# The recurrence's values by Strassen's scheme in a hybrid layer

## The chip, the core and the metric

One core of a Trainium2 chip runs the whole layer in one launch. It has a matrix engine (PE, with its weight loads shown as PEld), a vector engine (DVE), an activation engine (ACT), GpSimd (POOL), a queue engine that issues DMAs (SP), and 16 DMA engines. The metric is device microseconds from start to end, the median of several runs.

## The reference

The layer takes x of 512 tokens by 1024 channels, in float32. What matters here:

```python
h = rms_norm(x, norm_g); P = h @ W_in     # q | f | i | z_a | c_q | c_kv | k_rope | z_b | gates
f = lb + (1 - lb) * sigmoid(hf);  k = 1 - f;  v = hi            # hi = h @ W_I, 1024 columns
S_t = diag(f_t) S_{t-1} + k_t v_t^T;  o_t = S_t^T silu(q_t)     # 8 heads of 128, chunks of 32
y_a = rms_norm(o) * silu(z_a)
y_b = causal attention from the low-rank c_q, c_kv, k_rope, times silu(z_b)
m = sigmoid(g_a) * (y_a @ W_pa) + sigmoid(g_b) * (y_b @ W_pb)
out = rms_norm(x + m @ W_out)
```

The change concerns v = h @ W_I, a product of 512x1024 by 1024x1024.

## The kernel before

**Products.** Every operand of PE is split into a high and a low half (float32r), and a product is three matmuls into one bank of PSUM: hi by hi, hi by lo, lo by hi (`mm3`, L102 to L104). PE's left-hand data are h transposed, kept as two tiles `hT`. Weights come through `load_w` (L110 to L131): a DMA on SP's queue into one of three raw buffers, a cast to the high half on ACT (L129), a subtraction for the low half on DVE (L130); the high and low halves have four buffers each. PSUM's eight banks of 128x512 are two pools: three `mm` banks for projections and five `ax` banks for the rest.

**Stages.** RMS norm and transposes of x; the low-rank projections c, 256 columns during the norm and 448 after it (to 45 us); then four pairs of heads of the recurrence; then attention over eight heads; then the merge gates, the two projections and the output, which already use Strassen's scheme on 2x2 blocks (L898, L1096). For these, sums of weight blocks are made by DMA: `BlockSums` copies blocks in DRAM (`queued`, one copy behind each weight load) and adds others to them by accumulating DMAs on POOL (L800), one pair of them at each `step()`. Sums of token blocks of h are made by `early_sums` on DVE in pair 0 and saved to DRAM.

**A pair** (`hg_pair`) projects f for two heads (24 matmuls of 512 a head), and for each head runs `hg_forget`: tanh `tf` on ACT (L463), `f` on DVE (L464), `fr` and `k` on POOL (L465, L466), a scan (L468) and a reciprocal (L469) on DVE. The reciprocal takes the only buffer of `tf`, so the next head's `tf` must wait until `ki` (L486) has read it. `ko` (L487), `k64` on POOL (L488) and `k128` (L489) follow; `k128` is transposed on PE (L512) and used with the values for the states (L521, L522, L525). Then q's projection, scores (L535 to L546, masked on DVE at L550), outputs (L559, L561), the head's norm (L565 to L567) and the gate z_a. A pair with an even number first projects the values of four heads, 512 columns, by `proj_tok`: 4 token tiles of 8 x 3 matmuls, each tile copied by ACT (L603). So the values of all heads take 2 x 96 matmuls, in pair 0 and in pair 2.

**Order.** A scheduler in the framework orders each engine's instructions; each engine then runs its own list strictly in order. `tc.issue_after` holds an instruction behind another one. The low-rank tiles `c_sb` are transposed on PE (L425, 20 transposes into five ax banks), scaled by ACT (L426) and split by DVE (L427), within pair 0's forget projection.

## Time and profile before

| | us |
|---|---|
| median of 3 runs | 609.78 (609.2 to 610.34) |
| the profiled execution | 609.93 |
| its span | 607.7 |
| PE busy | 598.3 (98%) |
| DVE busy | 436.6 (72%) |
| ACT busy | 286.2 (47%) |
| POOL busy | 146.4 (24%) |

The difference between the profiled execution and its span, 2.2 us, lies outside the profiled instructions. Busy shares are means over stages. A row of the groups reads: line, engine, operation, out<-in with shapes, count, then busy time in us and the mean of one in ns, then the engine's idle time ahead of them and what ended it.

### The profile page before, as it was taken

What the parts mean: (1) busy time and instruction counts of PE and PEld (TensorE: products, weight loads), DVE (VectorE), ACT (ScalarE), POOL (GpSimd) and SP (SyncE); (2) the same over time, 40 slices, a digit from 0 to 9 for tenths busy, and PEclk for the clock granted to TensorE, in tenths of its full rate; (3) what the DMA queues carried; (4) which work ended last, traced back from release to release, by engine and by line L of the source; (5) the groups of instructions that cost most, each with busy time, mean ns of one, the idle gap of its engine ahead of it and who ended that gap; (6) DMA issues with size and microseconds to landing.
All of it is one profiled execution on the core that took longest, in us unless ns stands there. A gap on an engine that the chain in (4) does not pass through costs nothing.

```text
span 607.7 us, 9766 instructions
## 1 busy us (share of the span) xinstructions
PE 598.3 (98%) x3670; PEld 524.8 (86%) x3670; DVE 436.6 (72%) x684; ACT 286.2 (47%) x533; POOL 146.4 (24%) x253
## 2 busy tenths in 40 slices
PE   8999999999999999999999999999999999999995
PEld 5998888888888888888888888899999999888884
DVE  7717989599764548959767776747757678567886
ACT  6555245333313342435646555438757854424452
POOL 3106322254350137414254530400000000000012
PEclk9999999999999999999999999999999999999998
DMA  7549479987969967573369575866665564695113
GB/s 257 177 138 345 154 218 369 320 220 171 237 151 275 220 185 147 125 172 90 57 163 169 148 152 126 237 243 198 189 184 178 195 195 160 200 347 183 61 35 139
DMA packets 74543, 114.37 MB, mean 188 GB/s; under 512 B 7512, under 2 KB 41726, under 8 KB 74496
## 3 DMA queue, kind: packets, MB, share of 16 engines
q1 hardware_dynamic: 65244, 89.95, 46.1%
q0 software_dynamic: 8336, 22.55, 19.9%
q10 hardware_dynamic: 916, 1.25, 0.6%
q8 instruction: 29, 0.48, 0.3%
q14 instruction: 18, 0.15, 0.1%
HBM read 105.34 MB, written 39.85 MB: 239 GB/s over the span
## 4 chain that ended last, share of the span: by engine, by line
PE 96%; ACT 1%; DMA 1%; DVE 0%; issue 0%; SPq 0%; POOLq 0%; POOL 0%; ACTq 0%
PE mm_ps L102 19%; PE mm_ps L104 19%; PE mm_ps L103 19%; PE ax_ps L898 16%; PE ax_ps L1096 5%; PE mm_ps L898 3%; PE mm_ps L283 2%; PE ax_ps L757 1%; PE ax_ps L731 1%; PE ax_ps L559 1%; PE mm_ps L1096 1%; PE ax_ps L561 1%; PE ax_ps L521 1%; DMA w_raw<-w_in 1%; PE ax_ps L104 1%; PE ax_ps L103 1%
## 5 line engine op out<-in xcount | busy, mean ns | idle before, releaser
L130 DVE TENSOR_TENSOR w_lo<-w_raw,w_hi 128x1024 fp32r<-128x1024 f32 (+3 forms) x116 | 138.3, 1205 | 68.3 <-ACT w_hi L129 65.4
L129 ACT CAST w_hi<-w_raw 128x1024 fp32r<-128x1024 f32 (+3 forms) x116 | 115.1, 1005 | 130.1 <-PE mm_ps L103 56.5
L102 PE MATMUL mm_ps<-hT,w_hi 128*128 128x512 f32 x320 | 125.8, 394 | 0.0
L103 PE MATMUL mm_ps<-hT,w_hi 128*128 128x512 f32 x320 | 125.3, 391 | 0.0
L104 PE MATMUL mm_ps<-hT,w_lo 128*128 128x512 f32 x320 | 125.2, 393 | 0.0
L104 PEld LDWEIGHTS mm_ps<-hT,w_lo 128*128 128x128 f32 x320 | 60.1, 188 | 12.3
L102 PEld LDWEIGHTS mm_ps<-hT,w_hi 128*128 128x128 f32 x320 | 60.2, 188 | 11.9
L103 PEld LDWEIGHTS mm_ps<-hT,w_hi 128*128 128x128 f32 x320 | 60.2, 188 | 11.9
L898 PE MATMUL ax_ps<-s,w_hi 128*128 128x256 f32 x384 | 54.2, 283 | 0.2 <-ACT w_hi L129 0.2
L898 PEld LDWEIGHTS ax_ps<-s,w_hi 128*128 128x128 f32 x384 | 49.6, 192 | 0.5 <-ACT w_hi L129 0.5
L1147 POOL TENSOR_SCALAR ssum<-ssum 128x1 f32<-128x1 f32 x3 | 0.9, 309 | 188.0 <-ACT sq L1134 188.0
L103 PE MATMUL mm_ps<-w_lo,hT 128*128 128x512 f32 (+1 forms) x96 | 36.6, 383 | 0.0
L104 PE MATMUL mm_ps<-w_hi,hT 128*128 128x512 f32 (+1 forms) x96 | 36.5, 382 | 0.0
L102 PE MATMUL mm_ps<-w_hi,hT 128*128 128x512 f32 (+1 forms) x96 | 36.2, 386 | 0.0
L739 ACT ACTIVATE p<-ax_ps,sm 128x128 f32<-128x128 f32 (+3 forms) x32 | 16.7, 525 | 35.4 <-DVE sm L738 32.8
L741 POOL TENSOR_SCALAR p<-p,sm 128x128 f32<-128x128 f32 (+3 forms) x28 | 15.6, 560 | 66.2 <-DVE sm L740 54.9
L898 PE MATMUL ax_ps<-s,w_lo 128*128 128x256 f32 x192 | 31.4, 284 | 0.0
L469 DVE RECIPROCAL tf<-pr 128x512 f32<-128x512 f32 x8 | 26.8, 3348 | 0.1
L898 PEld LDWEIGHTS ax_ps<-s,w_lo 128*128 128x128 f32 x192 | 26.6, 192 | 0.2 <-DVE w_lo L130 0.2
L102 PE MATMUL mm_ps<-cT,w_hi 128*128 128x512 f32 x52 | 20.7, 397 | 0.0
L104 PEld LDWEIGHTS mm_ps<-w_hi,hT 128*128 128x128 f32 x96 | 18.0, 188 | 3.0
L102 PEld LDWEIGHTS mm_ps<-w_hi,hT 128*128 128x128 f32 x96 | 18.0, 188 | 2.9
(308 smaller groups left out, 1204.8 us busy)
## 6 DMA issues: line engine op xcount, KB each, us to landing
w_raw<-w_in SPq DMA_DIRECT2D x54, 512.0 KB, 6.4
g_t<-w_in SPq DMA_DIRECT2D x16, 512.0 KB, 9.1
w_raw<-g_t SPq DMA_DIRECT2D x16, 512.0 KB, 4.4
g_t<-w_in POOLq DMA_DIRECT2D x8, 512.0 KB, 10.5
pa_t<-w_proj_a SPq DMA_DIRECT2D x8, 512.0 KB, 8.9
g_t<-g_t POOLq DMA_DIRECT2D x8, 512.0 KB, 9.5
out_t<-w_out SPq DMA_DIRECT2D x8, 512.0 KB, 8.0
s<-h POOLq DMA_DIRECT2D x8, 512.0 KB, 11.6
```

What stands on the lines that cost most here:

```text
L102: nc.tensor.matmul(ps, lh[lsl], rh[rsl], start=start, stop=False)
L103: nc.tensor.matmul(ps, lh[lsl], rl[rsl], start=False, stop=False)
L104: nc.tensor.matmul(ps, ll[lsl], rh[rsl], start=False, stop=stop)
L129: last_hi[0] = nc.scalar.copy(hi[:, :o], raw[:, :o])
L130: last_lo[0] = nc.vector.tensor_tensor(lo[:, :o], raw[:, :o], hi[:, :o].bitcast(F32), op=ALU.subtract)
L283: nc.tensor.matmul(ps, hT[l][:, 4 * kh + k, t * P : t * P + P], c_hl[kh][r][:, k * 256 : k * 256 + 256], start=kh == 0 and kind == 0 and k ...
L469: nc.vector.reciprocal(rp[:], pr[:])
L521: nc.tensor.matmul(sps[:, sl], kt_[:, sl], v_sb[i][:, (h % 4) * P : (h % 4) * P + P], start=True, stop=True)
L739: last_act[0] = nc.scalar.activation(p[:, :n], sps[:, :n], AF.Exp, scale=SCALE, bias=sm[:, 1:2], accum_out=sm[:, 2:3])
L741: scaled_p = (nc.vector if final else nc.gpsimd).tensor_scalar(p[:, :n], p[:, :n], sm[:, 3:4], 0.5, op0=ALU.mult, op1=ALU.mult)
L898: nc.tensor.matmul(ps[:, o], w[k // 2][i][:, k % 2, cols], ap[j][:, k], start=not banks and c == 0 and n == 0, stop=n == 11, skip_group_ch ...
L1096: nc.tensor.matmul(ps[:, o : o + n], ap[i][:, k, t * P : t * P + P], w[k // 2][j][:, k % 2, o : o + n], start=fresh and c == 0, stop=c == ...
```

## The change

The values are one Strassen product now: seven products of 256x512 by 512x512, of 24 matmuls each (two token tiles, three kinds, four k), 168 instead of 192. W_I is taken in four blocks of 512x512, h in four blocks of 512 channels by 256 tokens. In pair 0 (`values_first`) there are five: U = h11 by I11; s2 by a sum of blocks and s3 by another, both added into U's banks; h12 by I21; h22 by a third sum. In pair 2 (`values_rest`) there are two: s1 by a fourth sum, then s4 by I22 into the same banks. The partial results that pair 2 needs are kept in four tiles (`v_late`). With this:

- Sums of W_I's blocks are made in SBUF, in the tile `ya` (which also holds x at the start): loads on SP, accumulating DMAs on POOL ahead of pair 0 and, for pair 2, in `RestSum` as the second step of pair 1.
- `early_sums` makes s2 and s3 on DVE ahead of the first forget projection; s1 and s4 are made in `fetch_rest`, behind pair 0's outputs on DVE.
- The first forget projection and U stand ahead of the transposes of `c_sb`, which are held behind U's first tile. The rope key's transposes move behind pair 0's states, and pairs 1 to 3 have their gate ahead of q's projection.
- Behind a weight load go up to two queued copies in pairs 0 and 1, one later, none in the last pair after its gate and at attention's first head. The block sums of the gates are added in another order, two steps a head for h > 4.

```diff
-                if queued:
+                for _ in range(min(len(queued), behind[0])):
...
+    i_w3, i_w2 = ya[:, 0:4], ya[:, 4:8]
...
+    for q in kh:
+        nc.gpsimd.dma_start(i_w3[:, q], i_w[1, 1][:, q], accum_op=ALU.add)
...
+    with tc.issue_after(c_lo_last.ins):
+        s_kept = early_sums()
+        for q in kh:
+            nc.vector.tensor_tensor(i_w2[:, q], i_w2[:, q], i_w3[:, q], op=ALU.add)
...
+    def v_product(ap, w, done, banks=None, tile=ax_tile):
+
+        res = banks or [tile() for _ in range(2)]
+        for t, ps in enumerate(res):
+            for n, (x, k) in enumerate((x, k) for x in range(3) for k in range(4)):
+                i, j = ((0, 0), (1, 0), (0, 1))[x]
+                mm_ = nc.tensor.matmul(ps[:], ap(i, k, t), w[k // 2][j][:, k % 2], start=not banks and n == 0, stop=n == 11,
+                                       skip_group_check=banks is not None)
...
+    first_f = proj_ch(w_in, COL_F, hT)
+    first_mm = []
+    first_u = v_product(h11, i_block(0, 0), lambda t, ps: first_mm.append(last_mm[0]))
...
-            nc.tensor.transpose(ps[:, t * P : t * P + P], c_sb[:, t, j * P : j * P + P], ident[:])
+            with tc.issue_after(first_mm[0].ins):
+                nc.tensor.transpose(ps[:, t * P : t * P + P], c_sb[:, t, j * P : j * P + P], ident[:])
...
+        for t, ps in enumerate(u):
+            nc.scalar.copy(v_sb[t][:], ps[:])
+        v_product(s2, i_split(i_w2), late(2), u)
+        v_product(s3, i_split(i_w3), late(3), u)
+        w10, raws = [], []
+        for q in kh:
+            w10.append(load_w(i_w[1, 0][:, q]))
+            nc.vector.tensor_tensor(i_w2[:, q], i_w2[:, q], last_raw[0].rearrange("p (k c) -> p k c", k=2), op=ALU.add)
+        v_product(h12, w10, lambda t, ps: nc.vector.tensor_tensor(v_sb[t][:], v_sb[t][:], ps[:], op=ALU.add), tile=mm_tile)
+        v_product(h22, i_split(i_w2), lambda t, ps: nc.scalar.copy(v_sb[2 + t][:], ps[:]), u)
...
+    class RestSum:
+
+        def add(self):
+            with tc.issue_after(last_pool[0].ins):
+                for q in kh:
+                    nc.gpsimd.dma_start(i_w2[:, q], i_w[0, 1][:, q], accum_op=ALU.add)
...
+    def values_rest():
+
+        def rest(n):
+            def done(t, ps):
+                nc.vector.scalar_tensor_tensor(v_sb[2 * (n - 2) + t][:], ps[:], -1.0, v_late[n, t][:], op0=ALU.mult, op1=ALU.add)
+            return done
+
+        r = v_product(of_sum(s_late[1]), i_split(i_w2), rest(3), tile=mm_tile)
+        v_product(of_sum(s_late[4]), i_block(1, 1), rest(2), r)
...
-            proj_tok(w_in, COL_I + cc, hT, lambda t, ps: nc.scalar.copy(v_sb[t][:], ps[:]))
-        else:
+            (values_rest if pair else values_first)()
+        if pair:
             zz = gate()
...
+    adds = [(gate_w[0], 0), (RestSum(),), (gate_w[0], 1), (gate_w[0], 2), (gate_w[0], 3), (gate_w[1], 0), (gate_w[1], 1),
...
         if pair == 0:
-            early_sums(kh[1])
+            with tc.issue_after(last_on[0].ins):
+                fetch_rest()
```

How the lists stand: three places, with the row's number, line, operation, out<-in. First ACT at the start of pair 0, before the change (`cT_91` is the scaled transposed low-rank tile, `v_821` to `v_824` the values).

```order
33 L129 CAST w_hi<-w_raw 128x1024 x2
34 L463 ACTIVATE tf<-mm_ps 128x512
35 L426 ACTIVATE cT_91<-ax_ps,par 128x512 x5
36 L129 CAST w_hi<-w_raw 128x1024
37 L171 CAST kpe<-ax_ps 128x512
38 L463 ACTIVATE tf<-mm_ps 128x512
39 L603 COPY v_821<-mm_ps 128x512
```

And the same place now (`ya` holds W_I's sums, `v_841` and `v_842` the values of two token tiles):

```order
37 L131 CAST w_hi<-w_raw 128x1024
38 L173 CAST w_hi<-ya 128x1024 x4
39 L526 ACTIVATE cT_91<-ax_ps,par 128x512 x5
40 L555 ACTIVATE tf<-mm_ps 128x512
41 L691 COPY v_841<-ax_ps 128x512
42 L691 COPY v_842<-ax_ps 128x512
43 L686 ACTIVATE qr<-ax_ps 128x512
```

The first tf moved from ahead of the five cT to behind them, and the copies of U's banks stand behind both. On PE the 48 matmuls of the forget projection and U's 24 now stand ahead of the 20 transposes, and the product of s2 into U's banks right behind them. On DVE four casts' low halves and two sums on `ya` stand ahead of the cT rows.

Second, POOL in pair 1 (`k_1390` and now `k_1433` are the second head's k64, `q_1536` and `q_1583` the first head's q64). Before:

```order
73 L488 TENSOR_TENSOR k_1390<-ko,gh_639 128x256
74 L800 DMA g_t_647<-w_in 128x2x512 x2
75 L502 TENSOR_TENSOR q_1536<-qi,gh_635 128x256
76 L502 TENSOR_TENSOR q_1545<-qi,gh_639 128x256
77 L800 DMA g_t_644<-g_t_643 128x1024 x2
```

Now:

```order
72 L594 TENSOR_TENSOR q_1583<-qi,gh_759 128x256
73 L580 TENSOR_TENSOR k_1433<-ko,gh_763 128x256
74 L713 DMA ya<-w_in 128x2x512 x2
75 L594 TENSOR_TENSOR q_1592<-qi,gh_763 128x256
76 L963 DMA g_t_768<-g_t_767 128x1024 x2
```

The accumulations of `RestSum` (L713) have the place that the second addition of the gates' sums had, behind the second head's k64.

Third, DVE in pair 2, whose rows between the low half of `RestSum`'s block (row 145) and the update of the values that the s4 product waits for (L742, `v_1854`) end so (`asb` are masked scores, `st` states):

```order
162 L642 COPY_PREDICATED asb_765<-mask_le,ax_ps 64x4x64
163 L617 SCALAR_TENSOR_TENSOR st<-st,ft,ax_ps 128x128
164 L132 TENSOR_TENSOR w_lo<-w_raw,w_hi 128x1024
165 L579 TENSOR_TENSOR ko<-ki,pr 128x512
166 L556 TENSOR_SCALAR f<-tf,c_425,c_427 128x512
167 L617 SCALAR_TENSOR_TENSOR st<-st,ft,ax_ps 128x128
168 L560 SCALAR_TENSOR_TENSOR pr<-f,fr 128x512
169 L561 RECIPROCAL tf<-pr 128x512
170 L742 SCALAR_TENSOR_TENSOR v_1854<-mm_ps,qh 128x512
171 L742 SCALAR_TENSOR_TENSOR v_1855<-mm_ps,p_917 128x512
```

Before, the values of pair 2 were four copies on ACT with nothing but casts between them:

```order
80 L463 ACTIVATE tf<-mm_ps 128x512
81 L603 COPY v_1805<-mm_ps 128x512
82 L603 COPY v_1806<-mm_ps 128x512
83 L129 CAST w_hi<-w_raw 128x1024 x3
84 L603 COPY v_1807<-mm_ps 128x512
85 L603 COPY v_1808<-mm_ps 128x512
```

The update of pair 2's values moved from ACT to DVE, where it stands behind the reciprocal of pair 2's second head (row 169). On PE the stretch from the s1 product to the s4 product holds the rest of pair 1 and the first tile of the next gate: 24 matmuls of s1, one head's states, the scores of pair 1, 24 matmuls of the gate and pair 1's outputs.

## The prediction

> **What bounds the kernel now.** First the page's busy shares and its chain that ended last, then what TensorE (PE) waited for, then the engines' busy time in the stretch that the change rebuilds (45 to 200 us).

> ```profile
> PE 598.3 (98%) x3670; PEld 524.8 (86%) x3670; DVE 436.6 (72%) x684; ACT 286.2 (47%) x533; POOL 146.4 (24%) x253
> PE 96%; ACT 1%; DMA 1%; DVE 0%; issue 0%; SPq 0%; POOLq 0%; POOL 0%; ACTq 0%
> PE ax_ps L248 <- DVE zero L294: 1.2, 1, 1.2
> ...
> PE ax_ps L898 <- ACT w_hi L129: 0.2, 1, 0.2
> ...
> 45.00:95.00 50.00, 50.00 (x240) 41.71 (x239) 43.38 (x57) 21.36 (x34) 19.97 (x34) 1.00 0.76 247
> 95.00:145.00 50.00, 50.00 (x311) 42.02 (x311) 40.95 (x50) 17.84 (x37) 19.20 (x36) 1.00 0.92 271
> 145.00:200.00 55.00, 55.00 (x342) 46.45 (x341) 37.44 (x45) 17.84 (x38) 18.89 (x38) 1.00 0.92 223
> ```

> A window row reads: length, then busy time of PE, PEld, DVE, ACT and POOL, the granted clock, the DMA engines' share. PE is the bound: 96% of the chain, and from 45 to 200 us it is busy in every microsecond. So a matmul that goes saves its whole pace, and any wait that is put in front of one costs its whole length. The second thing to see is the vector engine: 43.4 of 50, 41.0 of 50 and 37.4 of 55 us. In pairs 0 and 1 it is itself 82 to 87% full, so its queue has little room to be late in; and the DMA engines are 92% busy from 95 us on.

> **The saving.** The values cost 7 products of 24 matmuls instead of 192: 24 fewer of 128x512. Their pace stands in the chain of waits (start, length, what), as do the paces of the small products needed below:

> ```profile
> 562.41 5.44 PE ax_ps L1096 x24
> ...
> 54.57 2.18 PE ax_ps L425 x20
> ...
> 97.94 0.67 PE ax_ps L521 x6
> 104.55 1.08 PE ax_ps L535 x32
> 105.63 0.63 PE ax_ps L541 x32
> 106.26 1.07 PE ax_ps L546 x16
> 113.46 0.44 PE ax_ps L559 x4
> ...
> 116.36 0.22 PE ax_ps L561 x2
> ```

> 24 take 5.44 us (0.227 each). Without new waits: 609.93 - 5.4 = 604.5. Everything else is whether PE now waits. The groups that price it (busy us, mean ns):

> ```profile
> L129 ACT CAST w_hi<-w_raw 128x1024 fp32r<-128x1024 f32 (+3 forms) x116 | 115.1, 1005 | 130.1 <-PE mm_ps L103 56.5
> L130 DVE TENSOR_TENSOR w_lo<-w_raw,w_hi 128x1024 fp32r<-128x1024 f32 (+3 forms) x116 | 138.3, 1205 | 68.3 <-ACT w_hi L129 65.4
> L426 ACT ACTIVATE cT<-ax_ps,par 128x512 fp32r<-128x512 f32 x5 | 3.0, 692 | 1.0 <-PE ax_ps L425 1.0
> L427 DVE SCALAR_TENSOR_TENSOR cT<-ax_ps,par,cT 128x512 fp32r<-128x512 f32 x5 | 3.4, 722 | 0.0
> L463 ACT ACTIVATE tf<-mm_ps 128x512 f32<-128x512 f32 x8 | 4.8, 597 | 15.9 <-PE mm_ps L104 8.8 <-DVE ki L486 7.1
> L464 DVE TENSOR_SCALAR f<-tf,c,c 128x512 f32<-128x512 f32 x8 | 5.7, 710 | 2.0 <-ACT tf L463 2.0
> L465 POOL TENSOR_SCALAR fr<-f 128x16 f32<-128x16 f32 x8 | 3.9, 490 | 0.7
> L466 POOL TENSOR_SCALAR k<-tf,c1n,c 128x512 f32<-128x512 f32 x8 | 12.3, 1536 | 21.1 <-ACT tf L463 21.1
> L468 DVE TENSOR_TENSOR_SCAN pr<-f,fr 128x512 f32<-128x512 f32 x8 | 9.8, 1223 | 6.3 <-POOL fr L465 6.3
> L469 DVE RECIPROCAL tf<-pr 128x512 f32<-128x512 f32 x8 | 26.8, 3348 | 0.1
> L486 DVE TENSOR_TENSOR ki<-k,tf 128x512 f32<-128x512 f32 x8 | 5.5, 682 | 0.0
> L487 DVE TENSOR_TENSOR ko<-ki,pr 128x512 f32<-128x512 f32 x8 | 5.5, 687 | 0.1
> L488 POOL TENSOR_TENSOR k<-ko,gh 128x256 f32<-128x256 f32 x8 | 12.2, 1525 | 25.8 <-DVE ko L487 25.8
> L489 DVE TENSOR_TENSOR k<-ko,gh 128x512 f32<-128x512 f32 x8 | 6.3, 792 | 0.2
> L550 DVE COPY_PREDICATED asb<-mask_le,ax_ps 64x512 f32<-64x512 uint8 (+1 forms) x16 | 9.4, 587 | 0.8 <-PE ax_ps L546 0.6
> L525 DVE SCALAR_TENSOR_TENSOR st<-st,ft,ax_ps 128x128 f32<-128x128 f32 x16 | 5.3, 340 | 0.3
> L567 DVE TENSOR_TENSOR k<-ax_ps,ss x8: 685/692/693, 118.1 to 271.9; 128x512 f32<-128x512 f32 x8
> L603 ACT COPY v<-mm_ps 128x512 f32<-128x512 f32 x8 | 4.6, 586 | 11.6 <-PE mm_ps L104 11.4
> ```

> Rows of one engine overlap a little (five L427 of 722 ns are 3.4 us busy, some 0.06 each), which I take off.

> **Transposes behind the product U, 3.7 us.** Now they stood between the forget projection's matmuls and cost nothing beyond themselves. The change puts U (24 matmuls) ahead of them. U keeps two of the five ax banks, so of the five transposed tiles three fit; the fourth waits until the first is read by ACT (cT0) and DVE (cT1). On DVE cT1 stands behind the lo halves of the block i_w3, whose casts take the weight buffers that U frees: from the release 1.0 (L129) + 2 x 1.2 (L130) + 0.7 (L427) = 4.1 us. Meanwhile PE does U's last six matmuls and 12 transposes, 1.4 + 1.3 = 2.7, and U's last reads end some 0.2 late: 1.6 us of wait, then 0.2 for the fifth tile. The next product, s2, adds into U's own banks, so it waits until v0 is copied, and on ACT that copy stands behind the last cT0 and tf: 0.7 + 0.6 + 0.6 = 1.9. Nothing covers it: PE's next 36 matmuls all want those banks. Bounds 2 (one of the two waits overlaps the other) and 5.

> **The forget chain, 2.1 us.** Before, tf followed the projection and 192 matmuls hid the chain; now tf comes after the transposes. tf to the first turned keys: k 1.5 and fr 0.5 (one queue, POOL), scan 1.2, reciprocal 3.3, ki 0.7, ko 0.7, f 0.7, k128 0.8 = 9.4 and the semaphores between; PE has 0.6 + 42 matmuls (9.5): 0.3. The reciprocal writes the single buffer of tf, so the second head's tf waits for ki; behind it run k, k64, fr (1.5 + 1.5 + 0.5), scan 1.2, a lo half 1.2, reciprocal 3.3, and only then the lo half that the product of h12 needs, 1.2: 0.6 + 10.4 = 11.0 from ki, against PE's 2.2 + 0.3 + 32 x 0.227 = 9.8, near 1.0. Then ki, ko, k128 (2.2) against six matmuls (1.4): 0.8. Bounds 0 and 5 (POOL's rows vary). In pair 1 the query projection takes the bank of the second head's forget projection, which that head's tf frees, and tf waits for ki in a DVE queue that now carries sums: 0.4, between 0 and 1.5.

> **Pair 2, 9.1 us.** T is the moment when PE starts pair 0's outputs. From T to the s1 product PE has 169 matmuls of 512 (38.4), outputs (113.46 to 116.6: 3.1), 14 transposes (1.5) and one head's states (0.7): 43.7, with the 0.4 above T + 44.1. DVE begins after pair 0's outputs with their norm, T + 4.6 (first L567 118.1, less 113.46), and the sums s1 and s4 are put behind it. Up to the second head's ko stand 36 rows: two reciprocals 6.7, two scans 2.4, three lo halves 3.6, and 29 of 512 at some 0.69: 32.7, less 36 x 0.06 = 30.5; with 1.6 of waits for fr and the second norm T + 36.7. POOL then has k64 (1.5), and only behind it the accumulation that makes the block sum for s1: issued T + 38.2. What that DMA takes the trace does not show; the nearest rows:

> ```profile
> w_raw<-w_in SPq DMA_DIRECT2D x54, 512.0 KB, 6.4
> g_t<-w_in SPq DMA_DIRECT2D x16, 512.0 KB, 9.1
> ...
> g_t<-w_in POOLq DMA_DIRECT2D x8, 512.0 KB, 10.5
> ...
> qtab<-c_qtab POOLq DMA_DIRECT2D x1, 512.0 KB, 5.9
> DMA to landing us min/median/max: 5.5/9.8/14.0
> ```

> An accumulation from DRAM to DRAM lands in 10.5; a plain load to SBUF needs 2.7 less than a copy (9.1 against 6.4). I take 8.5, nearer to the only accumulation that is seen; ends 5.5 and 14.0 (the last row, all L800). So it lands T + 46.7 and is cast T + 47.7: PE waits 3.6 for w_hi.

> [...]

> From that cast to v2, which the s4 product needs (it reuses s1's banks), DVE has 26 rows: six lo halves 7.2, two reciprocals 6.7, two scans 2.4, four masks 2.3, six state rows 1.9, six of 512 at 0.7: 24.7 less 1.6 = 23. PE in the same stretch has 48 matmuls 10.9, states 0.7, scores 2.8, outputs 3.1 = 17.5. So v2 is ready at T + 70.7, PE without waits at T + 61.6: 9.1 in all, some of it taken at the gate's lo half that stands behind the first of these reciprocals. ZA's second tile can't fill in: s1's two banks and ZA's first are all three mm banks.

> **Costed at nothing.** The early sums run under the low-rank projection (45 to 61 us; if not, the forget's first lo half is 0 to 2 late). Copies two per load land long before the gates read them. From attention on PE's rows are the same and two steps a head for h > 4 add POOL issues beside a POOL that is 24% busy: 0 to 1.

> **Sum.** -5.4 + 3.7 + 2.1 + 0.4 + 9.1 = +9.9, on 609.93: 619.8; the median of the runs is 0.15 lower: 619.6.

> **Rivals.**
> (a) The accumulation lands fast, 5.5. For: its target is SBUF, plain loads take 5.9. Against: every accumulation shown but the fastest is slower. PE waits 0.6, v2 comes at T + 67.7: 6.1 in place of 9.1, 616.7. [...]
> (b) It lands late, 12 to 14, as DMA at 92% with two copies behind each load suggests: pair 2 costs 12.6 to 14.6, 623 to 625. Against: half its traffic stays off DRAM.
> (c) The vector engine keeps ahead. Place: pair 1's queue before the second head's ko. If its rows, sums included, are through by T + 27 instead of T + 36.7, the accumulation lands ahead of PE, the reciprocals run before s1, and pair 2's 9.1 is gone; the same lead in pair 0 takes the 2.5 of forget and bank. What stays starts from PE's own release of U: -5.4 + 3.7 = -1.7, 608.1, faster. It decides at v2 before T + 61.6. For: 37.4 of 55 us leaves DVE 17 free later on. Against: 41.0 of 50 before that, with 18 sum rows (12 us) added in one go.
> (d) Half of that: pair 2's wait goes, pair 0's stays: 609.93 - 5.4 + 6.2 = 610.7, 610.6 at the median: about no change.

> **Chances.** Forecast (617.5 to 622.5) 0.54, (a) 0.18, (b) 0.13, (c) 0.10, (d) 0.05. A measurement tells 0.2%, 1.2 us, from nothing. Faster 0.10, same 0.05, slower 0.85. Range 611 to 626: from (d)'s slow edge to (b) with another microsecond; the forecast's own is 614 to 624.

> **What would show it.** The waits view should have PE on L481 behind ACT's copy L691 (about 1.9), PE on L525 behind DVE's cT1, PE on L481 behind the cast of ya in pair 2 (about 3.6) and behind DVE L742. POOL's L713 should land 7 to 10 us after issue. If PE's list stays at 2 us in total, I am wrong and the time is near 604.5; if the pair 2 waits are absent, (c) or (d).

## The result and the profile after

The changed kernel takes 625.49 us (median of 6 runs, 623.18 to 628.81) against 609.87 (609.20 to 610.34, 6 runs) on the same chip: the ratio is 1.026, with an interval of 1.0228 to 1.0292. The forecast was 619.6: the sign was right, and the time lies inside the range of 611 to 626 but outside the forecast's own 614 to 624. Two executions of e7 below had a granted clock of 0.56 and 0.66 (987 and 841 us) and are left out of its figures.

The page's busy shares and its chain that ended last:

```profile
PE 601.8 (96%) x3646; PEld 524.5 (84%) x3646; DVE 458.9 (74%) x704; ACT 290.8 (47%) x539; POOL 154.2 (25%) x257
PE 79%; DVE 9%; DMA 4%; issue 2%; ACT 2%; POOL 1%; SPq 1%; POOLq 0%; ACTq 0%; DVEq 0%
```

PE has 24 matmuls fewer and is busy 3.5 us longer; the chain, which was PE to 96%, now runs through the vector engine and DMAs for an eighth of the span. What PE waited for (engine, tile, line, releaser: us in total, times, longest):

```profile
PE ax_ps L102 <- DVE k L659: 3.4, 1, 3.4
PE mm_ps L102 <- ACT tf L555: 2.4, 2, 1.2
PE ax_ps L481 <- ACT v L691: 1.7, 1, 1.7
PE ax_ps L1037 <- ACT w_hi L131: 1.6, 1, 1.6
PE ax_ps L525 <- DVE cT L527: 1.5, 1, 1.5
PE mm_ps L481 <- ACT w_hi L173: 1.4, 2, 0.8
PE mm_ps L481 <- DVE v L742: 1.3, 1, 1.3
...
PE ax_ps L604 <- DVE k L581: 0.4, 1, 0.4
PE mm_ps L481 <- ACT tf L555: 0.3, 1, 0.3
```

These are 14 us, where before had 0.2 in the gates and 0.6 for hT at the start; both kernels have 1.4 more at the start. The windows that answer to those shown of before (length, then PE, PEld, DVE, ACT, POOL, granted clock, DMA share):

```profile
45.00:95.00 50.00, 46.37 (x209) 37.66 (x208) 42.00 (x43) 21.92 (x33) 17.25 (x38) 0.97 0.46 147
95.00:145.00 50.00, 49.00 (x309) 41.06 (x307) 32.51 (x43) 16.66 (x34) 11.71 (x19) 1.00 0.84 253
145.00:200.00 55.00, 50.66 (x304) 41.19 (x305) 50.42 (x63) 18.05 (x37) 28.74 (x52) 0.97 0.69 179
```

Two things stand here. The vector engine went from 37.4 to 50.4 of 55 us in the last stretch, and from 41.0 to 32.5 of 50 in the one before it: its work has moved to where it is late. And the granted clock, 1.00 before, is 0.97 in two of the rows. It is one half for 3.41 us at a time, four times ahead of the last one at the end, which before has too (0.68 from 600 to 608 us there). Windows laid on those times (length, PE's busy time and matmuls, granted clock, DMA share; three pairs, each a stretch and the one behind it):

```profile
62.93:66.34 3.41, 1.31 (x8) 1.00 0.00 0
66.34:69.76 3.42, 2.96 (x7) 0.50 0.02 5
...
168.74:172.16 3.42, 1.85 (x6) 1.00 1.12 183
172.16:175.57 3.41, 3.41 (x10) 0.50 1.00 178
...
284.80:288.21 3.41, 1.27 (x6) 1.00 0.58 183
288.21:291.62 3.41, 3.41 (x12) 0.50 0.25 67
```

The fourth begins at 431.57, behind the wait in the gates. All four lie on one grid of 3.413 us: 66.34 + 31, 65 and 107 times 3.413 gives the others. Matmuls of 512 columns start there every 0.427 us, not every 0.227, so these stretches took a little under half their length from PE: by the starts 1.5 to 1.6 us each.

With the excess of each matmul's start over the pace of its kind, the 16.2 us between the two spans (623.9 less 607.7) lie so:

| place | forecast, us | measured, us |
|---|---|---|
| 24 matmuls less | -5.4 | -5.4 |
| transposes behind U, and U's copy (62 to 67 us) | 3.7 | 3.6 |
| forget chain, pair 0 | 2.1 | 0.5 |
| bank of the second forget projection, pair 1 (143.6) | 0.4 | 1.4 |
| pair 2 (168 to 193) | 9.1 | 4.95 of waits |
| attention's entry (283.2) | 0 | 3.55 |
| the gates (428.2), beyond before's 0.4 | 0 | 1.3 |
| four half-clock stretches | not seen | 6.2 |
| sum | +9.9 | +16.1 |

The table leaves out pieces that nearly cancel: 0.7 less at the start (the wait for hT), 0.4 less behind the last matmul, and some 1.2 of excesses under 0.2 each. It says where PE lost time, not what each place would give back: a PE that is late waits less at the next place.

### The profile page after: what moved, and what is told of

Same layout as the page of the kernel before. It is cut to its first block, busy times and chain, and to the rows that moved or that the text cites. A ratio compares the mean times of both kernels' runs of the same rounds, so it can differ in the third digit from the quotient of the medians.

```text
span 623.9 us, 9730 instructions
## 1 busy us (share of the span) xinstructions
PE 601.8 (96%) x3646; PEld 524.5 (84%) x3646; DVE 458.9 (74%) x704; ACT 290.8 (47%) x539; POOL 154.2 (25%) x257
## 4 chain that ended last, share of the span: by engine, by line
PE 79%; DVE 9%; DMA 4%; issue 2%; ACT 2%; POOL 1%; SPq 1%; POOLq 0%; ACTq 0%; DVEq 0%
PE ax_ps L1037 16%; PE mm_ps L102 13%; PE mm_ps L104 13%; PE mm_ps L103 13%; PE ax_ps L1237 5%; PE mm_ps L1037 2%; DVE tf L561 2%; PE mm_ps L481 2%; PE ax_ps L481 2%; PE mm_ps L287 2%; DMA w_raw<-w_uq 2%; DVE w_lo L132 1%; PE ax_ps L899 1%; DMA ya<-w_in 1%; PE ax_ps L925 1%
## 5 line engine op out<-in xcount | busy, mean ns | idle before, releaser
L132 DVE TENSOR_TENSOR w_lo<-w_raw,w_hi 128x1024 fp32r<-128x1024 f32 (+3 forms) x114 | 135.9, 1205 | 73.7 <-ACT w_hi L131 66.4
L131 ACT CAST w_hi<-w_raw 128x1024 fp32r<-128x1024 f32 (+3 forms) x114 | 112.4, 1004 | 131.0 <-PE mm_ps L103 32.1
L103 PE MATMUL mm_ps<-hT,w_hi 128*128 128x512 f32 x320 | 125.0, 391 | 0.0
L104 PE MATMUL mm_ps<-hT,w_lo 128*128 128x512 f32 x320 | 124.6, 390 | 0.0
L104 PEld LDWEIGHTS mm_ps<-hT,w_lo 128*128 128x128 f32 x320 | 60.1, 188 | 12.5
L103 PEld LDWEIGHTS mm_ps<-hT,w_hi 128*128 128x128 f32 x320 | 60.1, 188 | 11.8
L561 DVE RECIPROCAL tf<-pr 128x512 f32<-128x512 f32 x8 | 26.8, 3348 | 0.1
L594 POOL TENSOR_TENSOR q<-qi,gh 128x256 f32<-128x256 f32 x8 | 8.6, 1069 | 50.9 <-DVE qi L593 50.9
L104 PE MATMUL mm_ps<-cT,w_lo 128*128 128x512 f32 x52 | 20.9, 402 | 0.0
L102 PE MATMUL mm_ps<-cT,w_hi 128*128 128x512 f32 x52 | 20.9, 402 | 0.0
L103 PE MATMUL mm_ps<-cT,w_hi 128*128 128x512 f32 x52 | 20.6, 396 | 0.0
L1037 PE MATMUL ax_ps<-hT,w_hi 128*128 128x256 f32 x128 | 18.0, 283 | 0.0
L558 POOL TENSOR_SCALAR k<-tf,c1n,c 128x512 f32<-128x512 f32 x8 | 9.4, 1178 | 32.5 <-ACT tf L555 32.5
## 6 DMA issues: line engine op xcount, KB each, us to landing
w_raw<-w_in SPq DMA_DIRECT2D x52, 512.0 KB, 4.7
g_t<-w_in SPq DMA_DIRECT2D x16, 512.0 KB, 7.1
w_raw<-g_t SPq DMA_DIRECT2D x16, 512.0 KB, 4.6
g_t<-w_in POOLq DMA_DIRECT2D x8, 512.0 KB, 9.0
g_t<-g_t POOLq DMA_DIRECT2D x8, 512.0 KB, 10.2
pa_t<-w_proj_a SPq DMA_DIRECT2D x8, 512.0 KB, 10.6
out_t<-w_out SPq DMA_DIRECT2D x8, 512.0 KB, 6.5
s<-h POOLq DMA_DIRECT2D x8, 512.0 KB, 17.7
```

Source lines behind the costliest of these rows:

```text
L102: nc.tensor.matmul(ps, lh[lsl], rh[rsl], start=start, stop=False)
L103: nc.tensor.matmul(ps, lh[lsl], rl[rsl], start=False, stop=False)
L104: nc.tensor.matmul(ps, ll[lsl], rh[rsl], start=False, stop=stop)
L131: last_hi[0] = nc.scalar.copy(hi[:, :o], raw[:, :o])
L132: last_lo[0] = nc.vector.tensor_tensor(lo[:, :o], raw[:, :o], hi[:, :o].bitcast(F32), op=ALU.subtract)
L561: nc.vector.reciprocal(rp[:], pr[:])
```

## The experiments

Each starts from the changed kernel, unless it says otherwise, and is compared with the kernel before on the same chip.

**e1: U behind the transposes.** The product U is written behind the low-rank transposes, and these are not held.

```diff
-    first_u = v_product(h11, i_block(0, 0), lambda t, ps: first_mm.append(last_mm[0]))
...
-            with tc.issue_after(first_mm[0].ins):
-                nc.tensor.transpose(ps[:, t * P : t * P + P], c_sb[:, t, j * P : j * P + P], ident[:])
+            nc.tensor.transpose(ps[:, t * P : t * P + P], c_sb[:, t, j * P : j * P + P], ident[:])
...
-        u = first_u
+        u = v_product(h11, i_block(0, 0), lambda t, ps: None)
```

> Against the change alone one thing is moved: the product U is written behind the low-rank transposes, so these stand inside the forget projection again and do not share the ax banks with U. Theory (each wait is local to its place in the queues, and a stretch with about 1.5 us or more of idle costs another 1.7 us by a halved clock): the waits of 3.8 us at 62 to 67 us and the 1.6 us behind them go; in exchange U waits for two of the five banks to be read by the vector engine, up to 2.6 us. 620 to 623. Rival (the vector engine is simply too full, a wait that is taken away comes back at the next place): 624.5 to 625.5.

Measured: 620.76, ratio 1.0176 (1.0148 to 1.0204), 4.7 less than the change. The waits for L527 and L691 (1.5 and 1.7) are gone; U itself now waits 2.3 for a bank that holds a low-rank tile. So the edit saves some 1.3 us there, and most of the rest is the clock: no half-clock stretch follows U's wait at 57 us nor the one in the gates, two in place of four, 3.0 us.

**e2: saves and copies queued ahead of the values' products.**

```diff
     def values_first():
 
+        for n, hls in zip((2, 3), s_kept):
+            for q, hl in zip(kh, hls):
+                queued.append(lambda n=n, q=q, hl=hl: save(n, q, hl))
+        for w in (*gate_w, pa_w, out_w):
+            w.start()
...
```

(the same five lines go at its end)

> Against the change alone: the copies and saves are put in the list ahead of the values' products in pair 0 instead of behind them, so that two go with each of the loads there and none is left for pair 3. Theory (the 3.4 us wait at 283 us comes from copies between the weight loads of pair 3, which delay a load whose landing ACT's queue waits for, and with it the squares that free a bank): the wait and the halved clock behind it go, 5.3 us, and perhaps the 1.6 us with its clock at 428 us: 616.5 to 620. Rival (the wait at 283 us is set by the order of the engines, not by the copies): 625 to 626.

Measured: 621.47, ratio 1.0197 (1.0179 to 1.0215). That is 4.0 less than the change, and less than the theory's 616.5 to 620 promised; the rival's 625 fell. The two waits that the forecast had costed at nothing answer to this edit. The waits view of e2:

```profile
PE ax_ps L102 <- DVE k L659: 1.3, 1, 1.3
PE mm_ps L102 <- DVE z L673: 0.7, 1, 0.7
PE ax_ps L1037 <- ACT w_hi L131: 0.3, 1, 0.3
```

3.4 fall to 1.3 and 0.7 at the entry, 1.6 to 0.3 in the gates, and with them go the half-clock stretches at 288 and 432. The copies aren't the whole cause, though: e5, e9 and e10 below queue them early too, and e5 waits 1.6 in the gates, e9 1.8 and e10 2.8 at the entry.

**e3: pair 2's two products behind the gate.**

```diff
-            (values_rest if pair else values_first)()
+            if not pair:
+                values_first()
...
+        if pair == 2:
+            values_rest()
```

> Against the change alone: in pair 2 the two products are written behind the gate's projection instead of ahead of it. Theory (pair 2's loss is the sum of waits at the two products and at the gate between them: 2.1 for the accumulated block, 1.2 for the bank that the second head's tf holds, 1.3 for the update behind the reciprocal, and 1.7 of halved clock): these go, 618.5 to 620. Rival (the vector engine's rows are as many as before, so the same time is lost a little later, for the states of pair 2 need these values): 624 to 625.5.

Measured: 623.68, ratio 1.0227 (1.0212 to 1.0242), 1.8 less: the theory's 618.5 to 620 is missed, near the rival's 624. Pair 2's waits change their names and keep their size: 2.5 for DVE's k (L659), 1.1 for ACT's kt, 1.0 for tf, 0.5 for v (L742), together 5.1. PE does other work first and then waits for the same vector engine. One half-clock stretch is left of four, but new waits stand in place of the others, 0.3 and 1.0 at 83 to 86 us among them.

**e4 and e5: the three together.** U moreover goes into one mm and one ax bank (`u = [mm_tile(), ax_tile()]`), and the product of h12 into ax banks. In e4 `RestSum` is also first in the row of sums, and so it adds to `ya` (at 125 us) before the load that it should add to (at 132): the load overwrites it, and e4 leaves its block out of the fourth weight sum. In e5 it is second, as in the change, and nothing is left out.

> The three together, with the accumulation for pair 2 put first among pair 1's steps, and U in one mm and one ax bank so that it needn't wait for the transposes' banks; the product of h12 takes ax banks. Theory: the waits and the halved stretches go, and the 24 saved matmuls are seen: 604.5 to 607.5, below the kernel before. Rival (the vector engine is too full): above 610.

> The three parts of e1, e2 and e3 at once as in e4, but with the second pair's weight sum back in its place, second in the row of sums, so that nothing of the computation is left out. Theory (the waits the three parts leave are independent, and the clock falls only behind a stretch of 3.4 us that holds about 1.5 us of idle PE): the changed kernel has 625.5; without the transposes' 3.8, the 2.1 of attention's entry, the 1.7 of the gates and the 6.9 of four half-clock stretches it is 611, and what is left of pair 2's 5 us counts once more: 610 to 613, at most one half-clock stretch, in pair 2. Rival (VectorE is full in pairs 1 and 2, 34.7 of 35 us busy from 130 to 165, so what is taken away in one place comes back in pair 2): 615 as in e4, with over 6 us of waits there.

Measured: e4 615.55, ratio 1.0082 (1.0055 to 1.0110); e5 612.64, ratio 1.0052 (1.0033 to 1.0071). e4 missed its 604.5 to 607.5. In e5 the parts add up as its theory said (610 to 613), and the rival's 615 fell. But the waits left in pair 2 are still the vector engine's: in e5 PE waits 2.5 for k (L656) at 187 us, and a half-clock stretch follows.

**e6: the sums not held.** One edit alone, against the cause in pair 2:

```diff
         if pair == 0:
-            with tc.issue_after(last_on[0].ins):
-                fetch_rest()
+            fetch_rest()
```

> One part alone: the two token sums are no longer held until pair 0's outputs are issued, so VectorE may take them up in pair 0 already; all else as in the changed kernel. Theory (VectorE is busy 17.8 of 35 us from 95 to 130 and 34.7 of 35 from 130 to 165, so the sums lie in the wrong stretch): pair 2's waits fall from 4.95 us to under 2, the half-clock stretch at 172 goes with them, and the time falls by 4 to 7, to 618 to 622; VectorE's 95 to 130 rises towards 25 us or its 45 to 95 towards 47. Rival (pair 2 waits for RestSum's landing and for pair 2's own chain, not for the sums): the waits stay at 4 to 5 us, 624 to 626. Second rival (the sums push the forget chain of pair 0, where VectorE is already busy 42 of 50 us): over 1 us of new waits before 95, 623 to 625.

Measured: 614.21, ratio 1.0076 (1.0058 to 1.0095), 11.3 less than the change: the largest effect of one edit. Its windows (DVE's is the third busy figure, behind PE's and PEld's):

```profile
45.00:95.00 50.00, 46.63 (x206) 37.42 (x205) 46.16 (x52) 23.41 (x35) 18.84 (x38) 0.97 0.40 129
95.00:130.00 35.00, 35.00 (x246) 29.82 (x245) 24.54 (x37) 13.34 (x30) 4.15 (x6) 1.00 1.01 342
130.00:165.00 35.00, 34.27 (x184) 28.28 (x184) 25.92 (x29) 9.49 (x14) 18.42 (x33) 1.00 0.82 188
```

And what PE waits for in it behind 70 us:

```profile
PE ax_ps L102 <- DVE k L659: 0.8, 1, 0.8
PE ax_ps L613 <- ACT kt L605: 0.7, 1, 0.7
PE mm_ps L102 <- DVE z L673: 0.7, 1, 0.7
PE ax_ps L1036 <- ACT w_hi L131: 0.4, 1, 0.4
```

The vector engine takes up the sums in pair 0: 46.2 of 50 us in place of 42.0, then 24.5 of 35 in place of 17.8, and 25.9 in place of 34.7 from 130 to 165. Pair 2's 4.95 us fall to one wait of 0.7, the bank's 1.4 are gone, no wait before 95 us is added, and one half-clock stretch is left of four. The theory had 618 to 622: it had counted pair 2 and one stretch, but the bank, two more stretches and much of the later waits went as well (3.4 to 0.8 and 0.7 at the entry, 1.6 to 0.4 in the gates). Why the waits at the entry and in the gates fell, when their copies still stand where they stood, was not separated.

**e7 and e10: e5 and e6 together.**

> e5 and e6 together. Theory: the 24 matmuls that the change takes away are worth 5.4 us where nothing waits, so the 609.6 of before falls towards 604; waits of 1 to 3 us in pairs 0 to 2 and one in the gates (0.3 to 1.3) are left: 605 to 609, faster than before by 0.2 to 0.8 per cent, no half-clock stretch before the last 50 us. Rival (something in pair 2 that no edit so far has touched, such as the forget gate's own chain, needs 4 to 5 us more than before): 609 to 612, not faster than before.

Measured: ratio 1.0067 (1.0043 to 1.0092, four runs), some 613.5 us, against 605 to 609 expected: a miss. A second run of the same kernel, for a profile:

> e7's kernel once more, for a profile: e7 was expected at 605 to 609 and had 612.5 in its best runs. Theory (with pair 2's products behind the gate, VectorE's work for them stands in front of the next pair's, as in e3, whether the sums are early or not): 3 us or more of PE waits from 165 to 215 us, with a half-clock stretch behind them. Rival (h12's product in the ax banks holds up pair 0): the wait lies before 95 us. Second rival (attention's entry and the gates as in the changed kernel): over 4 us there.

It had 615.0 and these waits:

```profile
PE ax_ps L102 <- DVE k L656: 2.8, 1, 2.8
PE mm_ps L102 <- DVE f L588: 2.4, 1, 2.4
PE mm_ps L104 <- DVE w_lo L132: 2.1, 1, 2.1
```

In time they lie at 275 (the entry, with a half-clock stretch behind it), 208 (behind pair 2's products) and 86 us (behind the products of h12 and h22, where the next projection needs a low half). So there are waits at all three suspects' places. That moving pair 2's products puts vector work in front of the next pair, and that h12's product in ax banks holds up that low half, fits their places but isn't shown; the theory's 3 us or more from 165 to 215, with half clock behind, came as 2.8, without it.

**e9: what is left when these two are taken out again.** The sums free, copies early, U behind the transposes in one bank of each pool; pair 2's products and h12's banks as in the change.

> The changed kernel with three edits: the two token sums not held (e6), the saves and copies queued ahead of the values' products (e2), and U written behind the low-rank transposes into one bank of each pool (e5's form); pair 2's two products stay where the change has them. Theory (the waits are independent once VectorE has the sums early): e6's profile has a span of 612.0; from it go 1.7 and 1.9 at the transposes, the 1.7 that one half-clock stretch cost there, and about 1.9 at attention's entry; 0.9 in front of pair 2's gate and some 0.6 in the gates are left: a span of 605 to 606 and a time of 606 to 608, faster than before. Rival (the parts share VectorE, so what they save comes back, as it did in e7, which came out at 612.5 to 616 in its quicker runs): 610 to 614.

Measured: 608.54, ratio 0.9982 (0.9971 to 0.9992); the span is 606.3. It is the first to be faster than before, by 0.18%, about what a measurement can tell from nothing. The theory's 606 to 608 is missed by half a microsecond, since the wait at the entry didn't go. Whether h12's banks or the place of pair 2's products cost e7 more was not tried apart. The longest wait in e9's list:

```profile
PE ax_ps L102 <- DVE k L656: 1.8, 1, 1.8
```

And ScalarE's timeline ahead of it (start, length, operation, the idle time before it and its releaser):

```profile
263.29 0.58 ACT L811 COPY qr<-mm_ps 128x512 f32<-128x512 f32 x1
...
263.90 3.54 ACTq L813 DMA_DIRECT2D qs<-qr  x3
...
267.49 0.28 ACT L654 ACTIVATE osq<-ax_ps 128x128 f32<-128x128 f32 x1 [3.62 <-DMA qs<-qr]
```

Three small DMA issues take 3.54 us from the first to the last. Each of them is 0.52 long; the rest is two pauses between them. ScalarE's square sums of pair 3's outputs stand behind them; GpSimd's `ss`, the vector engine's `k` and PE's scores stand behind those. In the changed kernel the same row reads 3.71 us at 278.38, and the last square sums end at 286.3. SP's queue has the same trouble then: three issues of `w_raw<-w_uq` from 258.48 on took 3.98 us in e9.

**e12: that issue on GpSimd.** e9 with one line more:

```diff
-            nc.scalar.dma_start(qs[32 * b : 32 * b + 32, :], qr[32 * (b ^ 1) : 32 * (b ^ 1) + 32, :])
+            (nc.gpsimd if pair == 1 else nc.scalar).dma_start(qs[32 * b : 32 * b + 32, :], qr[32 * (b ^ 1) : 32 * (b ^ 1) + 32, :])
```

> e9 with one edit: the four copies of the turned queries (qs<-qr) of attention's second pair of heads, at its entry, are issued by GpSimd and not by ScalarE. In e9's profile ScalarE's sequencer spends 3.5 us on the first three of them (263.90 to 267.44), the square sums of the last output group (osq) stand behind them, GpSimd's ss, VectorE's k and PE's scores behind those: PE waits 1.8 us at 269.4, and the half-clock stretch from 271.6 costs another 1.7. Theory (that issue on ScalarE is what is late): GpSimd, idle there for 17 us, issues them in some 2.3 us; osq comes about 3.5 us earlier, the wait at the entry and the half-clock stretch are gone: 3 to 3.5 us off e9's 608.5, 605 to 606, faster than before by 0.6 to 0.8 per cent. Rival (the transfers in flight, not the engine, hold up the issue, so GpSimd stands there as long as ScalarE did, and its ss is late instead): the wait stays at 1.5 us or more, 608 to 609.

Measured: 604.94 (604.17 to 605.10), ratio 0.9917 (0.9904 to 0.9931): 0.8% faster than before. Its timeline, ScalarE's first square sum and GpSimd's issues:

```profile
264.90 0.28 ACT L654 ACTIVATE osq<-ax_ps 128x128 f32<-128x128 f32 x1
...
265.30 2.04 POOL L813 DMA_DIRECT2D qs<-qr  x4 [11.82 <-ACT osq L654]
```

And all of 0.3 us or more that PE still waits for behind the start, with the gates' wait:

```profile
PE ax_ps L610 <- ACT kt L602: 0.8, 1, 0.8
PE ax_ps L664 <- DVE k L656: 0.4, 1, 0.4
PE ax_ps L1034 <- ACT w_hi L131: 0.2, 1, 0.2
```

Four issues take GpSimd 2.0 us, osq starts 0.5 after qr's copy began in place of 4.2 after, and the granted clock is 1.00 in every window up to 560 us. The rival, that the transfers in flight would hold up any engine that issues, fell. What e12 gains on before is 4.7 us: of the 5.4 that 24 matmuls are worth, all but 0.7.

**e8 and e11: the clock by itself.** Both are the kernel before with stalls in the gates, where GpSimd has nothing to do. e8 has six, of growing length:

```diff
+    def stall():
+        ps = mm_tile()
+        nc.tensor.matmul(ps[:, :P], dl[:, :P], dl[:, :P], start=True, stop=True)
+        for n in stalls.pop(0):
+            nc.gpsimd.tensor_scalar(dl[:, :n], dl[:, :n], 1.0, 1.0, op0=ALU.mult, op1=ALU.mult)
+        nc.tensor.matmul(ps[:, P : 2 * P], dl[:, :P], dl[:, :P], start=True, stop=True)
```

> The kernel before with six stalls put into the gates, some 11 us apart, where GpSimd has nothing to do: a small matmul on a spare tile, one to three GpSimd passes over that tile, a second small matmul, so that PE stands idle for a set time. By rows of before (a GpSimd pass over 128x512 765 ns, x384 630, x256 475) and 0.5 for the way there and back the idle is about 0.8, 1.1, 1.5, 1.8, 2.0 and 2.5 us, 9.7 together, in this order. Theory (the granted clock falls to half for 3.4 us behind a stretch of 3.4 us that holds about 1.5 us of idle PE; the stretches run freely, so a stall that two of them share may pass): no half-clock stretch behind the first two, one behind at least two of the last four; 1.7 us for each beyond the idle itself: 609.8 + 9.7 + 3.4 to 6.8 = 623 to 626. [...]

Measured: 623.07. The six stalls were 0.45, 0.73, 1.95, 2.21, 2.38 and 2.92 us, and only the last was followed by half clock. On the grid that this half-clock stretch gives, the third and the last but one, and the last with what came behind it:

```profile
455.05:458.47 3.42, 1.71 (x15) 1.00 0.73 260
458.47:461.88 3.41, 3.17 (x27) 1.00 0.61 192
...
502.84:506.25 3.41, 1.94 (x17) 1.00 0.47 160
506.25:509.66 3.41, 3.41 (x31) 1.00 0.61 203
516.49:519.91 3.42, 0.81 (x7) 1.00 0.22 73
519.91:523.32 3.41, 3.41 (x18) 0.50 0.73 248
```

So the theory's mechanism stood and its size didn't: 1.5 us of idle is too low, since 1.84 in the stretch from 455.05 kept the clock. The fifth stall, longer than the third, was cut by the grid into 1.04 and 1.56 us. Neither transposes nor a crowded vector engine was needed for it: half clock follows a stall in the gates, far from any transpose, and the vector engine is busy 53.2 of 80 us from 440 to 520. That stall was one gap of 2.92 us. e11 puts the question between one long gap and a sum of short ones: six groups of four short stalls.

```diff
+        nc.tensor.matmul(ps[:], dl[:, :P], dl[:], start=True, stop=True)
+        for _ in range(4):
+            nc.gpsimd.tensor_scalar(dl[:], dl[:], 1.0, 1.0, op0=ALU.mult, op1=ALU.mult)
+            nc.tensor.matmul(ps[:], dl[:, :P], dl[:], start=True, stop=True)
```

> The kernel before with six groups of four short stalls in the gates: a 512-column matmul on a spare tile, then four times one GpSimd pass over it and the matmul again, so that PE stands idle four times for about 1.0 us with 0.23 us of work between, some 5 us in all. In the runs so far every stretch of 3.41 us (they lie on one grid in each profile) with 2.15 us or more of idle PE was followed by 3.41 us at half clock, and none with 2.14 or less was. Theory (the sum of idle time in a stretch of the grid decides): no idle above 1.3 us, and still half clock behind every group in which one stretch holds over 2.15 us, 3 to 6 of the six. [...]

Measured: 657.2, with half clock behind all six groups, for two stretches in five of them. The stalls were 0.8 to 1.2 us each, but for one of 1.8; five of the groups have none above 1.23. The row of the waits:

```profile
PE mm_ps L930 <- POOL dl L929: 25.2, 24, 1.8
```

And the windows of the first two groups, laid on the grid:

```profile
414.52:417.93 3.41, 0.86 (x3) 1.00 0.62 174
417.93:424.76 6.83, 5.84 (x26) 0.50 0.66 220
435.00:438.41 3.41, 0.89 (x3) 1.00 0.41 114
438.41:441.82 3.41, 2.77 (x13) 0.50 0.61 194
```

So in e11 the sum of idle time in one stretch of the grid counted, not the longest gap.

## Why the prediction was right or wrong

**The saving** of 5.4 us is real: e12, with nearly every wait gone, shows 4.7 of it.

**Transposes behind U**: right in size and mechanism. The waits named (L525 behind DVE's cT1, L481 behind ACT's copy L691) are those of the view; the excess over the pace is 1.7 and 1.9, forecast 1.8 and 1.9. e1 shows the cause: both go when U does.

**Forget chain of pair 0**: 0.5 in place of 2.1 (one wait for k128), but the chain was not much faster than forecast. The half-clock stretch ahead of it held PE back 1.5 us, and so PE came when the chain was nearly done. In e3 the clock doesn't fall there, and PE stands 0.4 for a low half and 1.2 for k128, 1.6 in all, and goes on no earlier: from the product behind U's copy to the transposes of k128 PE takes 19.2 us in both. So this term was right within half a microsecond, and the first half-clock stretch cost nothing in the end.

**The bank in pair 1**: the named wait came (`tf`, L555), with 1.4 for 0.4, inside the bound of 1.5.

**Pair 2**: the mechanism was right and so were its times; the difference between them was not. PE starts pair 0's outputs at T = 123.2. `RestSum`'s two DMAs by their line (durations of issue, first and last start, then issue to landing):

```profile
L713 POOL DMA_DIRECT2D ya<-w_in x2: 1271/1478/1685, 162.1 to 162.9; - x2
DMA to landing us min/median/max: 6.0/6.9/7.7
```

And PE's timeline where the s4 product begins:

```profile
193.25 0.50 PE L481 MATMUL mm_ps<-w_hi,qp 128*128 128x512 f32 x1 [1.34 <-DVE v L742]
```

Issued T + 38.9 (forecast 38.2), and v2 releases PE at 193.25, T + 70.0 (forecast 70.7). The landing, taken as 8.5, was 6.0 to 7.7, which put PE's wait ahead of s1's product at 2.1 in three pieces instead of 3.6 in one. PE, its waits taken off, came to v2 3.5 later than thought: 1.0 more in the bank of pair 1, 1.6 of half clock, 0.9 of small excesses. Waits of 4.95 and a half-clock stretch of 1.6 together are 6.55, for 9.1.

So what failed there is the size of two terms, the landing and PE's own delay. Rival (c), "the vector engine keeps ahead", was rightly held to be unlikely, but for a reason that failed: how full DVE was (41.0 of 50 us), as if that were fixed. But the sums were held behind pair 0's outputs, DVE was 17.8 of 35 us busy from 95 to 130, and e6 shows that the wait goes when the hold goes. The queue was late, not full.

**Costed at nothing**: wrong twice. "Copies two per load land long before the gates read them": the last of them went out at 213 us before and goes out at 315 now, so that they stand among the loads of attention. Before, then now (durations of an issue, first and last start):

```profile
L793 SPq DMA_DIRECT2D out_t<-w_out x8: 563/564/2294, 166.0 to 212.7; - x8
L954 SPq DMA_DIRECT2D out_t<-w_out x8: 563/564/1202, 272.3 to 315.0; - x8
```

They have a part in the waits at the entry (3.55) and in the gates (1.3), since e2 cuts both. They aren't needed for either: in e5 and e9 the last copy goes out at 256 and 252 us, and e5 still waits 1.6 in the gates and e9 1.8 at the entry; e6 leaves the copies where they are, and both waits shrink. "From attention on PE's rows are the same": they are, but what stands in front of the first of them had moved. e12 names the engine at the entry: ScalarE's DMA issue. In the gates ACT's cast waits 1.2 us for a landing of `w_raw<-g_t`, in the changed kernel as in e5; why that is late stays open.

**The price of a wait**: "any wait that is put in front of one costs its whole length" fell short. Where waits filled enough of a stretch of the clock's grid, they brought 1.5 to 1.6 us of slower matmuls with them, four times, and no term of the sum held that. In the table the four stretches are 6.2 us, nearly all that parts 16.1 from 9.9; the rest cancels, 5.8 too much in the forget chain and pair 2 against 5.9 too little at bank, entry and gates. But the rows are not independent. The first stretch only took the place of a wait for the chain, and the second stands ahead of v2, for which PE waits in any case. So how much of the 16.2 the clock alone costs isn't separated.

**The range**: that 625.49 lies inside it is in part luck. Its upper end, 623 to 626, was drawn for rival (b), an accumulation that lands after 12 to 14 us; this one landed after 6.0 to 7.7, and the time came there by the clock, the entry and the gates.

## What to carry to other kernels

When work is added to an engine, look at when it may start before you ask whether it fits: half-idle microseconds lay 30 us ahead of the stretch in which the sums were late. Every issue on a compute engine's queue, small DMAs included, is a place where that engine can stand (3.5 us in e9), so give it to an engine whose next work isn't due yet. And price several waits close together on PE above their sum, since the clock may fall for them, as it did for 2.24 us in pieces of at most 0.8 ahead of 172.16 in the changed kernel; but where the next place waits for another engine anyway, that extra may cost nothing.

## What was not expected of the hardware

| kernel | stretch | idle in it, us | half clock behind it |
|---|---|---|---|
| e11 | 414.5 to 417.9 | 2.87 | yes |
| e8 | 516.5 to 519.9 | 2.68 | yes |
| changed | 62.9 to 66.3 | 2.54 | yes |
| changed | 168.7 to 172.2 | 2.24 | yes |
| changed | 428.2 to 431.6 | 2.15 | yes |
| e9 | 268.2 to 271.6 | 1.95 | yes |
| e1 | 425.0 to 428.4 | 1.86 | no |
| e8 | 455.1 to 458.5 | 1.84 | no |
| e3 | 61.4 to 64.8, with 13 transposes | 1.91 | no |
| e3 | 64.8 to 68.2, with 3 transposes | 2.07 | no |
| e1 | 56.4 to 59.8, with 11 transposes | 2.14 | no |

Where only matmuls stand in the stretch, 1.86 us of idle in 3.41 kept the clock (e1) and 1.95 halved it (e9). Where transposes stand in it too, 2.14 was not enough, nor were 2.07 with three transposes and five matmuls; 2.54 with eight (the changed kernel at 62.9) was. With transposes the idle time is less surely known, and why the bound differs is open. e11's expectation had 2.15 as the bound; e9, which ran beside it, lowered it. In the changed kernel's stretch at 168.7 no single wait is above 0.8 us in the waits view, and in e11 gaps of at most 1.23 us in that view (1.4 by the starts), with work between them, halved the clock in five of the six groups: sums of small ones sufficed.

The second surprise is that three small DMA issues of ScalarE, 0.52 us each, kept the work behind them waiting for 3.5 us in e9: they start at 263.90, 264.97 and 266.93, with pauses between them (in the changed kernel at 278.38, 279.76 and 281.57). What the engine waits for in the pauses isn't settled: in e12 GpSimd issued the same four in 2.04 us, while SP's three issues of `w_raw<-w_uq` ahead of them took 3.94 us, as long as in e9.
